# A two-layer hybrid decoder: the last two pairs of a Strassen half multiplied ordinarily, the first up columns interleaved, the right half's chunks one block of K apart

## The chip, the cores and the metric

The kernel runs on one core of one Trainium2 chip. The metric is the device time of one execution in microseconds, 2214.55 in the median of three runs before the change (2214.05 to 2215.54). Engines are called as in the profile: PE is TensorE (matmuls, with PEld its weight loads), DVE is VectorE, ACT is ScalarE, POOL is GpSimd, SP is SyncE, which here only issues DMAs.

## The reference

Two layers, 256 tokens, width 2048, everything in float32. Each layer has a mixer (attention and a short gated convolution, one shared output projection) and an MLP. The change lies in the MLP and at its two ends:

```python
def reference(x, w_in, w_out, ..., w_up, w_down, rel_bias):
    for l in range(DEPTH):                       # 2
        h = _rmsnorm(x, attn_norm_g[l])
        proj = h @ w_in[l]                       # 2048 -> 6144
        ...                                      # attention and gated convolution
        x = x + jnp.concatenate([attn, conv], axis=-1) @ w_out[l]
        hm = _rmsnorm(x, mlp_norm_g[l]) @ w_up[l]             # 2048 -> 8192
        x = x + jnp.square(jax.nn.relu(hm)) @ w_down[l]       # 8192 -> 2048
    return x
```

## The kernel before

**Number format.** Every operand of a product is split into two rounded float32 parts, `hi` (made by ACT) and `lo` = value - hi (made by DVE). A product is three matmuls, hi.hi, hi.lo and lo.hi (`TERMS`). So each block of weights costs a DMA (SP queue), a `whi` or `uhi` on ACT and a `wlo` or `ulo` on DVE before PE can use it. A list of jobs does these (`Weights`): `take()` hands out the next one and makes jobs up to three ahead (`AHEAD`).

**Memory.** x stays in SBUF in four column chunks of 512 (`xs[0..3]`), each with two token tiles. Pools that are opened in a function are laid out in the order of opening and closed at its end; the next function's pools reuse the memory, and what is loaded there waits for the last reader of what lay there before. `mm` holds two PSUM tiles of two banks, `ps` three single banks (`bank`) and one named `av`.

**Order of work.** PE executes in the order of the program. On the other engines, and on the DMA queues, a scheduler orders the instructions by a simulated timeline, except those that `late` pins to their place in the program. Work beside the main stream (norms, transposes `tpn`, `nT`) is cut into pieces by generators (`work`), which advance at `tick()`.

**Mixer, `mixer`.** Projections by `linear` and `linear_t`, 512 output columns at a time, then the output projection "o" (four chunks n), after each of which x is updated (L658) and the MLP's norm is fed: `mnorm.chunk(n, 2)` transposes the chunk of x (`tpn`) and makes the two parts of it, `nT` (L247, L248). The last chunk, 3, is ready only some microseconds after the last matmul of "o".

**MLP, `mlp`.** DFF = 8192 is walked in 32 pairs (`NP`) of two 128-wide blocks of K. For pair i, two up columns (`up_column`, 64 matmuls) give h, [128, 4 blocks of 128]: two K blocks by two token tiles. `evict` adds their two halves, `square` applies relu, the norm's ratio and the square, stores the result to DRAM (`hid`, by the POOL queue), forms the Strassen sums S1 to S4 and splits all eight blocks into `f` (L805 hi, L806 lo). An up column needs all four chunks of `nT`: the first half of K (kh 0) chunks 0 and 1, the second half chunks 2 and 3.

The left half of the output columns (0 to 1023) is made by Strassen's products in Winograd's form, seven per pair of three matmuls 128x512 each instead of eight, accumulated in seven PSUM banks over all pairs. The products of pair j come two pairs (`LAG`) behind its up columns: after the first column of pair i the products of A11, A12, S4 and S1, after the second the other three. Their right-hand sides come from `quarters`: the raw rows of w_down (`draw`, 1024 KB per pair), the parts b1 and b2, the sums t (DVE, L724 to L728), and their parts t13 and t24 (L707 ACT, L708 DVE). All of these but b1 have one buffer.

After the last pair, the seven products are combined into x chunks 0 and 1 (`onto` and four adds, all on DVE). Then the right half (columns 1024 to 2047) is multiplied ordinarily: per pair the squared hidden is loaded back (`back`, 256 KB, SP queue), split (`fr`, L885 and L886), and 24 matmuls `dn` per K block run over both column chunks and both token tiles (L892). Both chunks end with the last pair; then x chunks 2 and 3 are updated and the next layer's norm or the output store follows. The next layer's first projection, q, starts on PSUM that the dn accumulators free.

## Time and profile before

| | |
|---|---|
| median of three runs | 2214.55 us (2214.05 to 2215.54) |
| the profiled execution | 2216.24 us |
| its span | 2214.4 us |
| its mean granted clock | 0.989 |
| matmul instructions | 11054 |
| DMA, mean over the span | 202 GB/s, 446.64 MB |
| `uraw`, 1024 KB, issue to landing | 5.8 us (median) |
| `draw`, 1024 KB | 5.1 us |
| `raw`, 512 KB | 3.6 to 3.9 us |
| `back`, 256 KB | 2.7 us |

The profile is of one execution. Its table of busy time says how long each engine worked; a row of digits per 40th of the span says how the granted clock of PE went; the chain of waits, followed back from the last instruction, says whose work set the end. The table of waits lists, for one engine, which instruction stood idle, for whom, for how long in all, how many times, and the longest. The timeline lists start, duration, engine, line, operation and tile, with the idle time before it and who ended it. The table by stage gives, for a stretch from:to, its length and then the busy time of PE, PEld, DVE, ACT and POOL with the number of instructions, then PE's granted clock, the DMA share and GB/s.

### The profile page before, as it was taken

Reading aid. Unit: us, or ns where it says so; the run is one execution under the profiler, and the core shown is the slowest. Engines: PE = TensorE matmul, PEld = TensorE weight load, DVE = VectorE, ACT = ScalarE, POOL = GpSimd, SP = SyncE. Lnnn points to the kernel's source line nnn. Section 1 sums busy time; section 2 is a strip of 40 time slices with the busy share of each in tenths; the row PEclk is TensorE's granted clock in tenths of the full one; section 3 lists DMA queues with packets and bytes.
Section 4 is the critical chain, followed back from the end, with each engine's and each line's share of the span. In section 5 each row is a group of like instructions: output and inputs, shape, how many; then the busy total and the mean of one; then the engine's idle time right before and its main releaser. Section 6 shows DMA issues by size and latency. Waiting matters only on the chain.

```text
span 2214.4 us, 29244 instructions
## 1 busy us (share of the span) xinstructions
PE 2167.4 (98%) x11054; PEld 1836.7 (83%) x11054; DVE 1631.7 (74%) x2303; ACT 1296.1 (59%) x1758; POOL 130.7 (6%) x186
## 2 busy tenths in 40 slices
PE   8999999999999999799999999999999999998999
PEld 6888888788888888688878888887888888886887
DVE  6677655789898989665556776557989898987555
ACT  6455445566666666454454654446666666664443
POOL 2021200000000000000010111000000000000000
PEclk9999999999999999899999999999999999998999
DMA  7656666566766666477565566656666666665774
GB/s 259 180 153 194 202 185 180 190 218 206 221 211 217 215 212 202 166 234 241 185 191 180 159 197 197 188 164 205 217 212 216 215 213 219 211 198 161 244 244 164
DMA packets 280717, 446.64 MB, mean 202 GB/s; under 512 B 10915, under 2 KB 191733, under 8 KB 280576
## 3 DMA queue, kind: packets, MB, share of 16 engines
q1 hardware_dynamic: 273872, 423.66, 61.7%
q0 software_dynamic: 6656, 21.10, 2.5%
q8 instruction: 86, 1.41, 0.3%
q14 instruction: 55, 0.45, 0.1%
q10 hardware_dynamic: 48, 0.02, 0.0%
HBM read 425.84 MB, written 18.90 MB: 201 GB/s over the span
## 4 chain that ended last, share of the span: by engine, by line
PE 96%; DMA 1%; DVE 1%; ACT 0%; issue 0%; POOL 0%; SPq 0%; DVEq 0%
PE dn L892 16%; PE pr L815 14%; PE o L337 8%; PE gc L359 4%; PE ci L359 4%; PE q L337 4%; PE gb L359 4%; PE v L337 4%; PE k L337 4%; DMA draw<-in_w_down_dram 1%; PE sc L499 1%; PE av L535 1%; PE tpn L401 0%; DVE wlo L282 0%; PE ptp L525 0%; PE up00b L776 0%
## 5 line engine op out<-in xcount | busy, mean ns | idle before, releaser
L282 DVE TENSOR_TENSOR wlo<-raw,whi 128x1024 fp32r<-128x1024 f32 (+1 forms) x258 | 317.1, 1231 | 244.3 <-ACT whi L281 243.1
L281 ACT ACTIVATE whi<-raw 128x1024 fp32r<-128x1024 f32 (+1 forms) x258 | 271.3, 1053 | 311.8 <-PE o L337 73.6
L692 ACT ACTIVATE uhi<-uraw 128x1024 fp32r<-128x1024 f32 x256 | 270.6, 1057 | 304.4 <-PE o L337 10.0
L693 DVE TENSOR_TENSOR ulo<-uraw,uhi 128x1024 fp32r<-128x1024 f32 x256 | 312.6, 1221 | 110.9 <-ACT uhi L692 106.7
L892 PE MATMUL dn<-whi,fr 128*128 128x512 f32 x1024 | 319.9, 393 | 9.5 <-ACT fr L885 7.0
L282 DVE TENSOR_TENSOR wlo<-draw,whi 128x1024 fp32r<-128x1024 f32 x128 | 156.9, 1225 | 150.7 <-ACT whi L281 150.6
L281 ACT ACTIVATE whi<-draw 128x1024 fp32r<-128x1024 f32 x128 | 135.7, 1061 | 174.4 <-PE dn L892 168.4
L892 PEld LDWEIGHTS dn<-whi,fr 128*128 128x128 f32 x1024 | 194.3, 190 | 51.4 <-ACT fr L885 7.9
L892 PE MATMUL dn<-wlo,fr 128*128 128x512 f32 x512 | 200.8, 392 | 0.0
L337 PE MATMUL o<-whi,cat 128*128 128x512 f32 x512 | 159.6, 390 | 0.0
L892 PEld LDWEIGHTS dn<-wlo,fr 128*128 128x128 f32 x512 | 97.2, 190 | 20.1
L337 PEld LDWEIGHTS o<-whi,cat 128*128 128x128 f32 x512 | 96.1, 188 | 19.8
L815 PE MATMUL pr<-t13h,f 128*128 128x512 f32 x256 | 100.5, 395 | 0.0
L337 PE MATMUL o<-wlo,cat 128*128 128x512 f32 x256 | 99.6, 389 | 0.0
L799 POOL DMA_DIRECT2D hid<-h x64 | 34.8, 544 | 985.4 <-ACT h L798 985.4
L815 PE MATMUL pr<-b2h,f 128*128 128x512 f32 x256 | 91.4, 398 | 0.0
L337 PE MATMUL q<-whi,nT 128*128 128x512 f32 x256 | 87.0, 409 | 3.3 <-ACT nT L247 2.1
L815 PE MATMUL pr<-t24h,f 128*128 128x512 f32 x256 | 89.6, 391 | 0.0
L337 PE MATMUL k<-whi,nT 128*128 128x512 f32 x256 | 85.3, 399 | 0.0
L337 PE MATMUL v<-whi,nT 128*128 128x512 f32 x256 | 83.4, 396 | 0.0
L708 DVE TENSOR_TENSOR t24l<-t,t24h 128x1024 fp32r<-128x1024 f32 x64 | 78.4, 1225 | 3.5 <-ACT t24h L707 0.4
L708 DVE TENSOR_TENSOR t13l<-t,t13h 128x1024 fp32r<-128x1024 f32 x64 | 78.4, 1224 | 3.5 <-ACT t13h L707 1.5
(953 smaller groups left out, 4667.8 us busy)
## 6 DMA issues: line engine op xcount, KB each, us to landing
uraw<-in_w_up_dram SPq DMA_DIRECT2D x128, 1024.0 KB, 5.8
draw<-in_w_down_dram SPq DMA_DIRECT2D x128, 1024.0 KB, 5.1
raw<-in_w_in_dram SPq DMA_DIRECT2D x192, 512.0 KB, 3.9
raw<-in_w_out_dram SPq DMA_DIRECT2D x64, 512.0 KB, 3.6
hid<-h POOLq DMA_DIRECT2D x64, 256.0 KB, 3.5
back<-hid SPq DMA_DIRECT2D x64, 256.0 KB, 2.7
rev<-by_dist_d POOLq DMA_DIRECT2D x4, 1024.0 KB, 10.6
out_dram<-x SPq DMA_DIRECT2D x8, 256.0 KB, 2.3
```

What stands on the lines that cost most here:

```text
L281: nc.scalar.activation(hi[:, k], raw[:, k], AF.Copy)
L282: nc.vector.tensor_sub(lo[:, k], raw[:, k], hi[:, k].bitcast(F32))
L337: nc.tensor.matmul(acc[:, t], a.ap[:, pa, k % KG, t * P:(t + 1) * P], (hi, lo)[pw][:, j], start=(k == 0 and n == 0), stop=(k == nk - 1 and ...
L359: nc.tensor.matmul(acc[:, f, 0] if part else acc[:, f], wt[:, k % 4, fs], a.ap[:, 0, k % KG] if part else a.ap[:, :, k % KG], start=(part ...
L499: nc.tensor.matmul(sc[:, :W], qT[m * DK:(m + 1) * DK, a, i, t * P:(t + 1) * P], kT[m * DK:(m + 1) * DK, b, i, :W], start=(n == 0), stop=(n ...
L535: nc.tensor.matmul(av[:, i * P:(i + 1) * P], pT[:, a, k * P:(k + 1) * P], v[:, b, k, i * P:(i + 1) * P], start=(k == 0 and n == 0), stop=( ...
L692: nc.scalar.activation(hi, src, AF.Copy)
L693: nc.vector.tensor_sub(lo, src, hi.bitcast(F32))
L708: nc.vector.tensor_sub(lo, src, hi.bitcast(F32))
L799: nc.gpsimd.dma_start(hid[i], u)
L815: nc.tensor.matmul(prods[n], f[:, pa, a], b[pw], start=(i == 0 and m == 0), stop=(i == NP - 1 and m == 2))
L892: nc.tensor.matmul(acc[n][:, t], f[:, pa, k, t * P:(t + 1) * P], b[pw][:, n], start=(i == 0 and k == 0 and m == 0), stop=(i == NP - 1 and ...
```

## The change

Three parts of `mlp` are changed, and with them the order in which its pools are opened.

1. The Strassen products take pairs 0 to 29 only. Pairs 30 and 31 are multiplied ordinarily, 48 matmuls for both, accumulated onto the banks of products 2, 4 and 3, which hold parts of one output block alone, and onto a free bank (product 8, the up columns' `av`). Their `f` has four blocks instead of eight, with no sums S1 to S4, and their rows of w_down go through `rows` and the ordinary weights, without t, t13, t24. Products 1, 5, 6 and 7 are combined while these matmuls run; four adds go from DVE to POOL.
2. The right half runs over 16 blocks of four K blocks (`NB2`), chunk n = 1 one block behind n = 0 (`order`). `hid` and `back` are 512 KB, the weights come as 512-column loads of 512 KB, as in the mixer, and each chunk's x update and norm start when it ends. The pools for it, `rpool` and `gpool`, are opened where `spool` and `upool` are closed.
3. Pair 0's two up columns run side by side, on one `mm` tile: first half of K for both, then the second half for both. Pair 1 uses two single banks, one for each column.

Besides, `fpool` and `dpool` are opened first, `spool` and `upool` last, and everything that `quarters(0)` makes on ACT and DVE after its DMA is pinned (`keep`).

```diff
-            upool = scope.enter_context(tc.tile_pool(name="upool", bufs=3))
-            spool = scope.enter_context(tc.tile_pool(name="spool", bufs=1))
             fpool = scope.enter_context(tc.tile_pool(name="fpool", bufs=2))
             dpool = scope.enter_context(tc.tile_pool(name="dpool", bufs=2))
+            first = scope.enter_context(ExitStack())
+            spool = first.enter_context(tc.tile_pool(name="spool", bufs=1))
+            upool = first.enter_context(tc.tile_pool(name="upool", bufs=3))
...
-            weights = Weights(upool)
+            weights = Weights(None)
...
+                keep = late if i == 0 else lambda ins: None
...
+                    keep(nc.scalar.activation(hi, src, AF.Copy))
+                    keep(nc.vector.tensor_sub(lo, src, hi.bitcast(F32)))
...
-                    nc.vector.tensor_sub(t[:, 0:2], raw[:, :, 1], raw[:, 0])
+                    keep(nc.vector.tensor_sub(t[:, 0:2], raw[:, :, 1], raw[:, 0]))
...
+                    keep(nc.vector.tensor_add(t[:, 2], t[:, 1], raw[:, 0, 0]))
+                    keep(nc.vector.tensor_sub(t[:, 3], raw[:, 1, 0], t[:, 2]))
...
-                        box.append(load_rows(i, 2 * CH))
+                        box.append(load_rows(i, 0))
...
-            for i in range(NP + LAG):
-                plain, sums, more = quarters(i - LAG)
-                if i < NP:
-                    column(i, 0, 0)
-                    column(i, 0, 1)
-                if i >= LAG:
-                    weights.jobs += [plain, sums]
-                if i < NP:
-                    column(i, 1, 0)
-                    column(i, 1, 1)
-                if i >= LAG:
-                    weights.jobs.append(more)
             for i in range(NP):
+                pair = quarters(i - LAG)
+                if i == 0:
+                    for kh in range(2):
+                        for c in range(2):
+                            column(0, c, kh)
+                    continue
+                for c in range(2):
+                    column(i, c, 0)
+                    column(i, c, 1)
+                    if i >= LAG:
+                        weights.jobs += (pair[2:], pair[:2])[c == 0]
+            for i in range(NP - LAG, NP):
                 box = []
                 rows(i, 0, box)
                 rows(i, 1, box)
...
-            hid = [dram.tile([P, 2 * S], F32, name=f"hid{l}{i}") for i in range(NP)]
-            def up_column(name, warm):
...
+            order = [(b - n, n) for b in range(NB2 + 1) for n in range(2) if 0 <= b - n < NB2]
+            for b, n in order:
+                weights.straight(w_down[l], b * KG * P, KG, (2 + n) * CH)
+            hid = [dram.tile([P, KG * S], F32, name=f"hid{l}{b}") for b in range(NB2)]
...
+                nc.gpsimd.dma_start(hid[i // 2][:, i % 2 * 2 * S:(i % 2 + 1) * 2 * S], u)
+                n = 4
+                if i < NP - LAG:
+                    n = 8
...
-                nc.vector.tensor_sub(f[:, 1], h, f[:, 0].bitcast(F32))
+                nc.scalar.activation(f[:, 0, :n], h[:, :n], AF.Copy)
+                nc.vector.tensor_sub(f[:, 1, :n], h[:, :n], f[:, 0, :n].bitcast(F32))
...
-            h = None
-            for i in range(NP + LAG):
+            for i in range(NP):
                 j = i - LAG
-                if i < NP:
-                    h = fpool.tile([P, 8, P], F32, tag="h", name="h", bufs=1)
-                    evict(up_column(f"up{l}{i}a", i < LAG),
-                          h[:, 0:2].rearrange("p a c -> p (a c)"))
...
-                if j >= 0:
-                    b11, b21, b22 = weights.take()
-                    t1, t3 = weights.take()
-                    product(0, j, A11, b11)
-                    product(1, j, A12, b21)
-                    product(2, j, S4, b22)
-                    product(4, j, S1, t1)
-                    work.tick()
-                if i < NP:
...
+                end = i == NP - 1
+                h = fpool.tile([P, 8, P], F32, tag="h", name="h", bufs=1)
+                if i == 0:
+                    two = mm.tile([P, 2, CH], F32, tag="mm2", name="up0")
+                    two = [two[:, c].rearrange("p (h s) -> p h s", h=2) for c in range(2)]
+                    for kh in range(2):
+                        for c in range(2):
+                            up_part(two[c], kh)
+                            if kh:
+                                evict(two[c], h[:, 2 * c:2 * c + 2])
+                    fs[0] = square(0, h)
+                    continue
+                for c in range(2):
+                    if i < LAG:
+                        acc = bank("upw").rearrange("p (h s) -> p h s", h=2)
+                    else:
+                        acc = column_bank()
+                    up_part(acc, 0)
+                    up_part(acc, 1)
+                    evict(acc, h[:, 2 * c:2 * c + 2])
+                    if c == 1:
+                        fs[i] = square(i, h)
+                    if j == 0 and c == 0:
+                        for pair in ((1, 6), (2, 3)):
+                            w2 = mm.tile([P, 2, CH], F32, tag="mm2", name=f"pr{l}{pair[0]}")
+                            prods[pair[0]], prods[pair[1]] = w2[:, 0], w2[:, 1]
+                        for n in (4, 5, 7):
+                            prods[n] = bank(f"pr{l}{n}")
+                    if j >= 0 and c == 0:
+                        b11, b21, b22 = weights.take()
+                        t1, t3 = weights.take()
+                        product(1, j, A11, b11, end)
+                        product(2, j, A12, b21)
+                        product(3, j, S4, b22)
+                        product(5, j, S1, t1, end)
+                        work.tick()
+                    elif j >= 0:
+                        t2, t4 = weights.take()
+                        product(7, j, S3, t3, end)
+                        product(6, j, S2, t2, end)
+                        product(4, j, A22, t4)
+                        work.tick()
+            first.close()
+            rpool = scope.enter_context(tc.tile_pool(name="rpool", bufs=RAW))
+            gpool = scope.enter_context(tc.tile_pool(name="gpool", bufs=3))
+            weights.pool = rpool
+            def block(b):
+                back = gpool.tile([P, KG * S], F32, tag="back", name="back", bufs=2)
+                nc.sync.dma_start(back, hid[b])
+                f = gpool.tile([P, 2, KG, S], F32R, tag="g", name="g")
+                flat = f.rearrange("p a k s -> p a (k s)")
+                nc.scalar.activation(flat[:, 0], back, AF.Copy)
+                nc.vector.tensor_sub(flat[:, 1], back, flat[:, 0].bitcast(F32))
+                return f
+            blocks = {0: block(0)}
...
-            e1 = wide("e1")
-            nc.scalar.activation(e1, p1, AF.Copy, scale=mnorm.scale)
-            onto(xs[0][:, 0], p2, xs[0][:, 0])
-            onto(xs[1][:, 0], p3, xs[1][:, 0])
-            onto(xs[0][:, 1], p4, xs[0][:, 1])
-            u2, u3, u4 = wide("u2"), wide("u3"), wide("u4")
-            onto(u2, p6, e1)
-            onto(u3, p7, u2)
-            onto(u4, p5, u2)
-            onto(xs[1][:, 1], p5, xs[1][:, 1])
-            for dst, v in ((xs[0][:, 0], e1), (xs[1][:, 0], u4), (xs[0][:, 1], u3),
-                           (xs[1][:, 1], u3)):
-                nc.vector.tensor_add(dst, dst, v)
+            x11, x21, x12, x22 = (xs[n][:, t] for n in range(2) for t in range(NT))
+            e1, e2, e3, e4 = wide("e1"), wide("e2"), wide("e3"), wide("e4")
+            nc.scalar.activation(e1, prods[1], AF.Copy, scale=mnorm.scale)
+            onto(e2, prods[6], e1)
+            onto(e4, prods[5], e2)
+            onto(x22, prods[5], x22)
+            onto(e3, prods[7], e2)
+            for dst, v in ((x11, e1), (x12, e4), (x21, e3), (x22, e3)):
+                nc.gpsimd.tensor_tensor(dst, dst, v, op=ALU.add)
+            prods[8] = ps.tile([P, CH], F32, tag="av", name=f"pr{l}8", bufs=1)
+            for j in range(NP - LAG, NP):
+                for k in range(2):
+                    b = weights.take()
+                    for n, t, p in ((0, 0, 2), (0, 1, 4), (1, 0, 3), (1, 1, 8)):
+                        for m, (pa, pw) in enumerate(TERMS):
+                            nc.tensor.matmul(
+                                prods[p], fs[j][:, pa, 2 * k + t], b[pw][:, n],
+                                start=(p == 8 and j == NP - LAG and k == 0 and m == 0),
+                                stop=(j == NP - 1 and k == 1 and m == 2))
+                    work.tick()
+            for dst, p in ((x11, 2), (x21, 4), (x12, 3), (x22, 8)):
+                onto(dst, prods[p], dst)
...
             if last:
-                for n in range(2):
-                    for t in range(NT):
-                        nc.sync.dma_start(
-                            out[0, t * P:(t + 1) * P, n * CH:(n + 1) * CH], xs[n][:, t])
+                store(0)
+                store(1)
             else:
                 work.start(norm.chunk(0, 2), 12)
...
-            acc = [mm.tile([P, NT, CH], F32, tag="mm2", name=f"dn{l}{n}") for n in range(2)]
-            for i in range(NP):
-                back = nat.tile([P, 2, S], F32, tag="wide", name="back")
-                nc.sync.dma_start(back.rearrange("p k s -> p (k s)"), hid[i])
-                f = fpool.tile([P, 2, 2, S], F32R, tag="f", name="fr")
-                nc.scalar.activation(f[:, 0], back, AF.Copy)
-                nc.vector.tensor_sub(f[:, 1], back, f[:, 0].bitcast(F32))
-                for k in range(2):
-                    b = weights.take()
-                    for n in range(2):
+            accs = {}
+            for b, n in order:
+                if n == 0:
+                    if b + 1 < NB2:
+                        blocks[b + 1] = block(b + 1)
+                if b == 0:
+                    accs[n] = mm.tile([P, NT, CH], F32, tag="mm2", name=f"dn{l}{n}")
+                f, acc = blocks[b], accs[n]
+                for kp in range(KG // 2):
+                    hi, lo = weights.take()
+                    for k in (2 * kp, 2 * kp + 1):
                         for t in range(NT):
                             for m, (pa, pw) in enumerate(TERMS):
                                 nc.tensor.matmul(
-                                    acc[n][:, t], f[:, pa, k, t * P:(t + 1) * P], b[pw][:, n],
-                                    start=(i == 0 and k == 0 and m == 0),
-                                    stop=(i == NP - 1 and k == 1 and m == 2))
+                                    acc[:, t], f[:, pa, k, t * P:(t + 1) * P],
+                                    (hi, lo)[pw][:, k % 2],
+                                    start=(b == 0 and k == 0 and m == 0),
+                                    stop=(b == NB2 - 1 and k == KG - 1 and m == 2))
                         work.tick()
-            for n in range(2):
-                for t in range(NT):
-                    onto(xs[2 + n][:, t], acc[n][:, t], xs[2 + n][:, t])
+                if b == NB2 - 1:
+                    for t in range(NT):
+                        onto(xs[2 + n][:, t], acc[:, t], xs[2 + n][:, t])
                     if last:
-                        nc.sync.dma_start(
-                            out[0, t * P:(t + 1) * P, (2 + n) * CH:(3 + n) * CH],
-                            xs[2 + n][:, t])
-                if not last:
-                    work.start(norm.chunk(2 + n, 2))
+                        store(2 + n)
+                    else:
+                        work.start(norm.chunk(2 + n, 2))
```

## The prediction

> **What bounds the kernel now.** I read the page first: which engine is busy, and whether its clock ever drops.
>
> ```profile
> PE 2167.4 (98%) x11054; PEld 1836.7 (83%) x11054; DVE 1631.7 (74%) x2303; ACT 1296.1 (59%) x1758; POOL 130.7 (6%) x186
> PEclk9999999999999999899999999999999999998999
> PE 96%; DMA 1%; DVE 1%; ACT 0%; issue 0%; POOL 0%; SPq 0%; DVEq 0%
> ```
>
> TensorE carries the end (96% of the chain). Time is lost only where PE waits, and just after, when its granted clock is low (the 8s). So next the waits of PE (total, times, longest):
>
> ```profile
> PE pr L815 <- ACT f L805: 9.8, 2, 5.0
> PE dn L892 <- ACT fr L885: 7.0, 2, 5.6
> PE up00a L776 <- DVE nT L248: 4.7, 2, 3.7
> PE up10a L776 <- DVE nT L248: 4.6, 2, 3.6
> PE tpn L401 <- DVE nT L248: 3.0, 1, 3.0
> PE dn L892 <- DVE fr L886: 2.5, 1, 2.5
> PE pr L815 <- DVE t24l L708: 2.3, 2, 1.1
> ```
>
> Almost all lie at three places per layer: the first up columns, the end of the left half, the layer boundary. The table by stage (from:to, length, then PE busy; the clock stands after POOL):
>
> ```profile
> 398.97:418.27 19.30, 14.60 (x75) 12.39 (x74) 17.33 (x28) 12.07 (x19) 0.89 (x2) 0.82 0.83 272
> 905.41:940.02 34.61, 22.86 (x74) 16.88 (x72) 23.79 (x32) 16.07 (x24) 0.54 (x1) 0.75 0.58 203
> 1111.39:1141.34 29.95, 25.85 (x115) 21.31 (x115) 16.52 (x25) 15.27 (x26) 3.32 (x5) 0.94 0.68 211
> 1502.01:1520.91 18.90, 14.35 (x76) 12.18 (x74) 17.20 (x28) 12.09 (x19) 0.89 (x2) 0.91 0.83 278
> 2008.04:2038.04 30.00, 19.66 (x64) 14.12 (x63) 22.83 (x31) 12.44 (x15) 0.54 (x1) 0.77 0.56 177
> ```
>
> Everywhere else (940.02 to 1111.39: busy 171.37 of 171.37, clock 1.00) PE is full. Unit prices at full clock: 0.2267 us per 128x512 matmul (612 dn in 138.75 us). After an idle of some 5 us (918.64, 932.52, 2021.50) matmuls start 0.43 us apart for 5.7 to 6.3 us, which loses about 2.9 us; after 2.5 to 3.7 us of idle, 1 to 1.5 us.
>
> **1. Tail of the left half: -17.3 and -14.5 us.** From the last up matmul of layer 1 to its last dn matmul the trace has 905.41 to 1111.39, 205.98 us. Content: 9+21+21 = 51 product matmuls, 768 dn, 16 transposes of 0.1 = 11.6 + 174.1 + 1.6 = 187.3. So 18.7 us are lost: waits of 1.14, 4.80, 0.25 and 5.55, and about 7 at low clock. In layer 2, 201.59 against 185.7 (no transposes): 15.9 lost. The change makes pairs 30 and 31 cost 48 matmuls instead of 42, +1.4 us, and takes the sums and the 1024-wide `f` out ahead of them. I count from T, the last up matmul: nine products end at 2.05, pair 30 lasts to 7.5. Meanwhile ACT does `ev` 0.58, `e1` 0.58, relu and square 0.62 each, half an `f` hi 0.6; DVE, in the built order, `h` 0.4, `e2`, the ratio, `e4`, `x22`, `e3` (0.75 each) and half an `f` lo, 0.68: ready at about T+6, 1.5 before pair 31. The SP queue can't issue `back` and the first right-half weights before the last Strassen product (their buffers reuse its memory): T+2.25; 512 KB land in 3.6 to 3.9; `g` hi 6.5 to 7.5, the last `whi` of pair 31 to 8.5, its `wlo` 8.7 to 9.9, needed at 10.2 to 10.5. First right-half weights: ready 11.05, needed 12.97. So nothing waits, if those landings hold; gain 18.7 - 1.4 and 15.9 - 1.4. Were the dn wait to stay with its slow clock (5.55+2.9), -9 would remain per layer: the other bound.
>
> Four adds go to POOL, and POOL can cost DVE time:
>
> ```profile
> 233.78 1.29 POOL L645 TENSOR_TENSOR gc02w<-gc02w,rowb 128x512 f32<-128x512 f32 x1
> 234.10 2.05 DVE L282 TENSOR_TENSOR wlo<-raw,whi 128x1024 fp32r<-128x1024 f32 x1 [0.83 <-ACT whi L281]
> ```
>
> A `wlo` that takes 1.22 alone takes 2.05 beside a 1.29 us POOL operation. POOL's last add would run till T+8.3, beside `g` lo: +0.8, so pair 31's last `wlo` ends at 10.7 and not 9.9, and PE waits 0.3: +0.3 per layer (bounds 0 and 1.9, all four at 0.83 less the 1.5 of slack). The Trainium skill (GPSIMD Engine Reference, Specifications) puts such contention on DVE instructions with two SBUF inputs; then `e2` to `e3`, which read PSUM, are spared. The trace agrees: a 0.68 us add from PSUM at 232.59 kept 0.68 beside a POOL operation. Were they not spared, `f` lo would be 2.5 us later, and each layer would pay 1 more.
>
> **2. Right half one block apart: -6.0 us, once.** In layer 1's boundary, 29.95 us hold waits of 1.10 (PSUM of q, behind the x update of 2.72) and 3.00 (`tpn` for nT), 4.1, and 1.9 of low clock. Chunk 0 now ends a block (48 matmuls, 10.9 us) before chunk 1, and so do its x update, its norm pieces and its PSUM. The next q's first weights can be issued at the last `wlo`, some 6.6 us before the last dn; landing 3.8, `whi` 1.06, `wlo` 1.22: ready 0.5 early. Content remains: -6.0 (bounds 0, if that 0.5 fails, and -6.0). At the end of the kernel the last x update and store remain: 0.
>
> **3. First up columns side by side: +4.4 and +4.7 us.** The order of columns alone would hide the wait for nT chunk 3:
>
> ```profile
> 398.97 1.98 PE L776 MATMUL up00a<-nT,uhi 128*128 128x512 f32 x8
> 404.69 0.50 PE L776 MATMUL up00a<-nT,uhi 128*128 128x512 f32 x1 [0.98 <-DVE nT L248]
> 408.91 1.65 PE L776 MATMUL up00a<-nT,uhi 128*128 128x512 f32 x3 [3.72 <-DVE nT L248]
> 399.21 0.88 SPq L699 DMA_DIRECT2D draw<-in_w_down_dram  x2
> 393.73 1.06 ACT L692 ACTIVATE uhi<-uraw 128x1024 fp32r<-128x1024 f32 x1 [1.66 <-PE o L337]
> ```
>
> Waits 0.98 + 3.72 and 2.4 at low clock: 7.15 of 19.30, so content 12.15 (layer 2: 6.75 of 18.90). But the diff also reverses the pools. In before, `uraw` lies where the mixer's bias lay, is loaded at 205 us, and `uhi` is made at 393.73, under the o projection; it is `draw` that waits for the last o matmul (399.21). In the built program of the changed kernel `dpool` and `upool` have swapped places: `uraw` overlaps the mixer's `cat`, and its first DMA waits for the last o matmul. All SP issues behind it wait too, the next two `uraw` among them. So: issue 399.2, landing 6.2 (as the draw issued there; bounds 5.4, the fastest, and 8.4, the median of uraw at 395 to 425), `uhi` 1.06, first up matmul 406.5 instead of 398.97: 7.6 us idle, 2.9 of low clock, 0.8 because column 1 ends in the tile that column 0's eviction reads, 0.2 for nT: 12.15 + 11.5 = 23.65 (layer 2 alike), against 19.30 and 18.90. Bounds +2.3 and +6.6.
>
> **4. Pair 0's quarters pinned: +9.9 us in each layer.** `t` and `t13` of pair 0 were made at 405 to 411 us, far ahead of use. `keep` now holds them in program order, and in the built order DVE's `t` stands behind `b2l` and `f` lo of pair 1. `b2l` needs `b2h` of pair 1 (one buffer), which waits for pair 0's product 3. But `t13` is needed directly after product 3. From X, the end of up column 2a: product 3 ends 2.2, `b2h` 3.3, `b2l` 4.5, `f` lo 5.6, `t` 6.9, `t13h` 7.95, `t13l` 9.2. PE, in order, waits from 2.05 to 7.98 and again to 9.2, and the next up column starts at 9.7 and not 2.73: 7.0 idle and 2.9 of low clock. DVE and ACT, held up likewise, catch up in the slow stretch. Bounds: 7.0 (no low clock) and 11 (`t24` late too).
>
> The 2.9 is a row. The Trainium skill (TensorE: Matmul & The Clock Gate, Part 1) has the gate release after one busy window of about 3.4 us at half rate, 1.7 lost per idle: the four new idles would then cost 4.8 less, 2201. The trace has 5.7 to 6.3 us.
>
> **Sum.** -17.3 - 14.5 + 0.6 - 6.0 + 4.4 + 4.7 + 9.9 + 9.9 = -8.3. The profiled execution took 2216.24 (span 2214.4): 2207.9. The median of the runs is 2214.55, 1.7 lower: 2206.
>
> **Rivals.**
> (a) Neither start stall comes (the reused memory and the pinned order bite nowhere). For it: none of these waits is in this trace. Against it: both orders stand in the built program. Then part 4 is 0 and part 3 is -6.3 and -5.9 (the waits less 0.85): 2216.2 - 37.2 - 12.2 - 1.7 = 2165.
> (b) One of the two comes: without part 4, 2206 - 19.8 = 2186; without part 3's late uraw, 2206 - 21.3 = 2185.
> (c) Slower than before: the right half becomes bound by transfers. Its weights now come in rows of 512 columns instead of 1024. A layer's right half moves 33.5 MB of weights and 8.4 of hidden in 174.1 us, 241 GB/s. Loads of such rows ran at 179 GB/s with a DMA share of 0.63 (1141 to 1160), full share 284; the present ones at 217 with 0.68, full 319. That speaks against it, with 0.85 of the limit used. It decides below 41.9/(174.1+6.4) = 232 GB/s, where the two layers' extra passes 8.3 + 4.4; at 230 it costs 8.1 per layer, 2222.
> (d) The change does not do what it says, the tail's waits return (`back` late): -9 per layer, 2206 + 14 = 2220.
>
> **How the numbers follow.** Forecast 0.55, own range 2195 to 2218 (gate and landing low; landing high and one tail wait). (a) 0.10, (b) 0.17, (c) 0.10, (d) 0.08. Two of ten may fall outside 2182 to 2224: it leaves out (a) and the far ends of (c). No change means within 0.2%, 4.4 us, which a measurement here can just tell: under 2210.1 is faster, over 2219 slower. Faster: 0.40 of the forecast's 0.55, (a), and nearly all of (b): 0.65. Slower: (c), most of (d), little of the forecast: 0.17. Same: 0.18.
>
> **What would show it.** Part 1: no PE wait on `f` or `g` behind the last up column, at most 0.3 on a `wlo`. Part 2: no wait on nT between the layers. Part 3: first `uraw` issued right behind the last o matmul, first up matmul waiting some 7.6 us for `uhi`. Part 4: product 5 of pair 0 waiting about 6 us for `t13h` and 1.2 for `t13l`. A wait of dn on `whi` or `raw` all through the right half means (c). If `uraw` loads before the last o matmul, or if `t13` is ready in time, I am wrong by 20 us.

## The result and the profile after

The changed kernel takes 2212.18 us in the median of 16 runs (2209.88 to 2214.07), beside 2215.67 in 16 runs of the kernel before (2214.05 to 2218.11) on the same chips. The ratio is 0.9984, 95% interval 0.9976 to 0.9991. So it is faster by 3.5 us, 0.16%: clear of zero by the interval, but inside the 0.2% that the prediction called no change (its line for faster was 2210.1), an outcome to which it gave 0.18. The profiled execution took 2213.11, with a span of 2211.3; the forecast for it was 2207.9.

Span by stage. "Front" is the end of the o projection to the end of pair 0's two up columns (64 matmuls), "loop" reaches to the last up column, "tail" to the last dn matmul. "Boundary" is the start of the next layer's q projection, its first 96 matmuls, up to the first k:

| stage | before | after | forecast | measured |
|---|---|---|---|---|
| start | 398.97 | 398.26 | 0 | -0.7 |
| front, layer 1 | 19.30 | 24.85 | +4.4 | +5.6 |
| loop, layer 1 | 487.14 | 497.70 | +9.9 | +10.6 |
| tail, layer 1 | 205.98 | 190.85 | -17.0 | -15.1 |
| boundary | 29.95 | 23.15 | -6.0 | -6.8 |
| mixer 2 | 360.67 | 360.82 | 0 | +0.2 |
| front, layer 2 | 18.90 | 25.47 | +4.7 | +6.6 |
| loop, layer 2 | 487.13 | 497.11 | +9.9 | +10.0 |
| tail, layer 2 | 201.59 | 188.13 | -14.2 | -13.5 |
| end | 4.77 | 4.96 | 0 | +0.2 |

The measured column adds up to -3.1, the difference of the spans. Each stage moved the way that was forecast for it; some 36 us were won and 33 were lost. On the page the shares of the engines have hardly changed, and PE still carries the chain; "issue" has 4% of it, where before it had none:

```profile
PE 2163.5 (98%) x11066; PEld 1835.1 (83%) x11066; DVE 1610.7 (73%) x2229; ACT 1286.7 (58%) x1718; POOL 137.8 (6%) x194
PEclk9999999999999999999999999998999999999999
PE 94%; issue 4%; DMA 1%; DVE 0%; POOL 0%; ACT 0%; SPq 0%; DVEq 0%; POOLq 0%
```

The waits of PE after (total, times, longest) tell more than the shares:

```profile
PE up L789 <- ACT uhi L694: 18.5, 2, 9.6
PE pr L829 <- ACT t13h L714: 11.5, 2, 5.8
...
PE pr L829 <- DVE t13l L715: 3.1, 2, 2.0
PE q L338 <- ACT nT L248: 2.7, 1, 2.7
PE pr L916 <- DVE wlo L283: 1.5, 2, 0.8
PE up L789 <- ACT ev L799: 1.4, 2, 0.7
```

None of the seven waits shown of before is left: `f`, `fr`, the `nT` at the front and the `tpn` at the boundary are gone, but for 0.2 us at the front. (The `q` wait on `nT` is at the start of the kernel.) In their place stand two waits per layer that before did not have: the first up column on `uhi`, and pair 0's fifth product on `t13`.

The stages by window after (from:to, length; busy time of PE, PEld, DVE, ACT, POOL with counts; granted clock, DMA share, GB/s):

```profile
398.26:423.11 24.85, 15.03 (x75) 12.42 (x75) 11.76 (x20) 10.31 (x16) 0.89 (x2) 0.79 0.75 240
436.90:460.00 23.10, 16.23 (x69) 13.15 (x69) 17.87 (x24) 10.86 (x14) 0.56 (x1) 0.78 0.50 153
920.81:934.86 14.05, 13.29 (x59) 10.63 (x58) 13.16 (x13) 8.46 (x11) 5.64 (x5) 1.00 0.74 268
934.86:1111.66 176.80, 176.80 (x793) 146.63 (x792) 102.57 (x97) 89.56 (x102) 0.00 (x0) 1.00 0.72 229
1111.66:1134.81 23.15, 23.15 (x108) 19.22 (x106) 14.65 (x20) 12.23 (x18) 3.35 (x5) 1.00 0.90 298
```

The tail and the boundary (the last three rows) are now all but full: PE waits 0.76 us in them, at clock 1.00. The first two rows are where the gain went: the front, with a clock of 0.79, and the stretch around pair 0's products, where PE now waits and the clock is 0.78.

The front in the timeline (start, length, engine, line, operation; in brackets the idle time before it and what ended it), SP and ACT first, then PE:

```profile
398.49 16.50 SPq L687 DMA_DIRECT2D uraw<-in_w_up_dram  x5
...
406.28 2.00 ACT L694 ACTIVATE uhi<-uraw 128x1024 fp32r<-128x1024 f32 x2 [5.77 <-DMA uraw<-in_w_up_dram]
...
398.03 0.39 PE L338 MATMUL o<-whi,cat 128*128 128x512 f32 x1
407.39 3.78 PE L789 MATMUL up<-nT,uhi 128*128 128x512 f32 x8 [8.98 <-ACT uhi L694]
...
420.21 2.12 PE L789 MATMUL up<-nT,uhi 128*128 128x512 f32 x8 [0.69 <-ACT ev L799]
```

The first `uraw` is issued right behind the last o matmul, as forecast, and lands 7.7 us later. And pair 0's products in layer 1:

```profile
443.23 1.22 DVE L715 TENSOR_TENSOR b2l<-draw,b2h 128x1024 fp32r<-128x1024 f32 x1 [0.86 <-ACT b2h L714]
444.37 1.22 DVE L821 TENSOR_TENSOR f<-h,f 128x1024 fp32r<-128x1024 f32 x1
445.51 1.22 DVE L728 TENSOR_TENSOR t<-draw 128x1024 f32<-128x1024 f32 x1
...
446.76 1.06 ACT L714 ACTIVATE t13h<-t 128x1024 fp32r<-128x1024 f32 x1 [2.62 <-DVE t L728]
...
447.87 0.79 PE L829 MATMUL pr<-t13h,f 128*128 128x512 f32 x1 [5.76 <-ACT t13h L714]
449.76 0.80 PE L829 MATMUL pr<-t13l,f 128*128 128x512 f32 x1 [1.10 <-DVE t13l L715]
450.78 3.62 PE L789 MATMUL upc<-nT,uhi 128*128 128x512 f32 x8
```

`t` is the third in DVE's queue, behind `b2l` and `f` lo of pair 1, and PE stands for 5.76 and 1.10 us in front of `t13h` and `t13l`. The prediction wrote these steps as offsets from the start of pair 0's products, X, which is 439.87 here: `t13h` needed from X+2.05 and there at X+7.98, which is 447.85.

### The profile page after: what moved, and what is told of

It is laid out like the page before. It is cut to its first block, busy times and chain, and to the rows that moved or that the text cites. A ratio compares the mean times of both kernels' runs of the same rounds, so it can differ in the third digit from the quotient of the medians.

```text
span 2211.3 us, 29293 instructions
## 1 busy us (share of the span) xinstructions
PE 2163.5 (98%) x11066; PEld 1835.1 (83%) x11066; DVE 1610.7 (73%) x2229; ACT 1286.7 (58%) x1718; POOL 137.8 (6%) x194
## 3 DMA queue, kind: packets, MB, share of 16 engines
HBM read 425.84 MB, written 18.90 MB: 201 GB/s over the span
## 4 chain that ended last, share of the span: by engine, by line
PE 94%; issue 4%; DMA 1%; DVE 0%; POOL 0%; ACT 0%; SPq 0%; DVEq 0%; POOLq 0%
PE upc L789 30%; PE dn L950 16%; PE pr L829 13%; PE o L338 8%; PE q L338 4%; PE gc L360 4%; PE ci L360 4%; PE gb L360 4%; PE v L338 4%; PE k L338 4%; PE sc L500 1%; PE av L536 1%; DMA hid<-h 1%; DMA raw<-in_w_down_dram 1%; PE tpn L402 1%
## 5 line engine op out<-in xcount | busy, mean ns | idle before, releaser
L283 DVE TENSOR_TENSOR wlo<-raw,whi 128x1024 fp32r<-128x1024 f32 (+1 forms) x386 | 473.4, 1227 | 384.2 <-ACT whi L282 382.8
L282 ACT ACTIVATE whi<-raw 128x1024 fp32r<-128x1024 f32 (+1 forms) x386 | 407.2, 1055 | 481.1 <-PE dn L950 163.6
L789 PE MATMUL upc<-nT,uhi 128*128 128x512 f32 x1920 | 480.2, 392 | 0.0
L789 PEld LDWEIGHTS upc<-nT,uhi 128*128 128x128 f32 x1920 | 354.9, 189 | 69.0
L950 PE MATMUL dn<-whi,g 128*128 128x512 f32 x1024 | 316.3, 389 | 0.0
L789 PEld LDWEIGHTS upc<-nT,ulo 128*128 128x128 f32 x1920 | 262.8, 191 | 18.8
L789 PE MATMUL upc<-nT,ulo 128*128 128x256 f32 x1920 | 268.5, 283 | 0.0
L950 PEld LDWEIGHTS dn<-whi,g 128*128 128x128 f32 x1024 | 192.2, 188 | 40.0
L950 PE MATMUL dn<-wlo,g 128*128 128x512 f32 x512 | 199.2, 389 | 0.0
L950 PEld LDWEIGHTS dn<-wlo,g 128*128 128x128 f32 x512 | 96.1, 188 | 19.8
L829 PE MATMUL pr<-t13h,f 128*128 128x512 f32 x240 | 95.1, 396 | 11.5 <-ACT t13h L714 11.5
```

The source lines that it names most:

```text
L282: nc.scalar.activation(hi[:, k], raw[:, k], AF.Copy)
L283: nc.vector.tensor_sub(lo[:, k], raw[:, k], hi[:, k].bitcast(F32))
L789: nc.tensor.matmul(acc[:, 0] if part else acc, wt[:, k], a.ap[:, 0, k % KG] if part else a.ap[:, :, k % KG], start=(part == 0 and kh == 0 ...
L829: nc.tensor.matmul(prods[n], fs[j][:, pa, a], b[pw], start=(j == 0 and m == 0), stop=(stop and m == 2))
L950: nc.tensor.matmul(acc[:, t], f[:, pa, k, t * P:(t + 1) * P], (hi, lo)[pw][:, k % 2], start=(b == 0 and k == 0 and m == 0), stop=(b == NB2 ...
```

## The experiments

Every run was timed beside the kernel before in the same group; ratios are to that kernel, with 95% intervals. Diffs are against the changed kernel. The expectations, which were written before each run, call the runs by short names, in the order of the work: e1 is the pin taken away, e2 the old layout of the pools with the pin left in, e3 and e4 both undone (columns side by side, then one after the other), e5 pair 0 one pair earlier, e6 two `uraw` buffers, e7 the adds on DVE, e8 the chunks in the same block, e9 and e11 another layout in both orders, e10 the draws held back, e12 both stalls avoided.

### The pin of pair 0 taken away

```diff
-                keep = late if i == 0 else lambda ins: None
+                keep = lambda ins: None
```

> The changed kernel without `keep`: pair 0's quarters may be made ahead again. My theory (product 5 of pair 0 waits 5.8 and 1.1 us for t13 in the changed kernel, and the stretch from pair 1's first column to the end of the last up column is 10.6 and 10.0 us longer than before): both waits go, the stretch returns to some 487 us per layer, and the time is about 20 us below the changed kernel, 24 below the kernel before (2192). Rival: the wait belongs to the one buffer of b2 and t13, and comes back somewhere in the first pairs: within 5 us of the changed kernel.

2194.39 us, ratio 0.9903 [0.989, 0.9917]. Both waits on `t13` are gone. The loops take 487.13 and 487.14, as before the change; fronts 25.03 and 26.25 and tails 190.83 and 188.10 stay. So the pin costs 10.6 and 10.0 us a layer, and buys nothing in this layout, where the first `uraw` is late anyway. (Of these 20.6 us, 17.8 reached the median: the start of this profiled run was 1.5 us longer and its second front 0.8.)

### The pools laid out as before, the pin left in

```diff
-            fpool = scope.enter_context(tc.tile_pool(name="fpool", bufs=2))
-            dpool = scope.enter_context(tc.tile_pool(name="dpool", bufs=2))
+            fpool = scope.enter_context(tc.tile_pool(name="fpool", bufs=2, side="right"))
+            dpool = scope.enter_context(tc.tile_pool(name="dpool", bufs=2, side="right"))
...
-            spool = first.enter_context(tc.tile_pool(name="spool", bufs=1))
             upool = first.enter_context(tc.tile_pool(name="upool", bufs=3))
+            spool = first.enter_context(tc.tile_pool(name="spool", bufs=1))
```

> The changed kernel with `upool` and `spool` laid where the kernel before has them and `fpool`, `dpool` at the other end of the memory: the first `uraw` loads no longer reuse the mixer's `cat`. `keep` stays. My theory: the first up matmul follows the last o matmul at once, the front falls from 24.9 and 25.5 us to about 13.2 each, and the time is about 24 us below the changed kernel, 27 below the kernel before (2188). Rival: the idle at the front is due to nT chunk 3 and the norm as before: the front keeps some 19 us, and the time falls by 12 at most.

2206.73 us, ratio 0.9957 [0.9944, 0.9971]. The fronts fall to 14.85 and 14.55, 10 and 11 us less: the late `uraw` is the layout's doing. But only 5.5 us of the 21 reached the end, so the theory's 2188 was missed; the total fell by no more than the rival's 12, though not for its reason, a front that stays at 19. The boundary grew to 32.80 (+9.65), with a new 5.3 us wait of `q` on `whi`: the same pools, closed at the end of the left half, decide what memory the right half gets, and its `back` and `g` now lay over the next mixer's first weight buffers, whose load therefore waited for the last dn. Tails grew by 1.1 each, loops by 2. The layout only moved the wait to another place.

### Both undone, and the columns one after the other

The first of these has both edits above. The second, besides, walks the columns in the order of before:

```diff
-                    for kh in range(2):
-                        for c in range(2):
+                    for c in range(2):
+                        for kh in range(2):
```

> Both edits at once: no `keep`, and `uraw` in its old place. If the two stalls are separate, their gains add: 44 us below the changed kernel, 48 below the kernel before (2168). Rival: without the pin, pair 0's sums get ahead of the first columns' `ulo` on DVE as soon as these are early, and the front gives back 2 to 5 us per layer: 2172 to 2178.

> As e3_both, with pair 0's two up columns one after the other again (first c, then kh). My theory: the second half of K of the first column then waits for nT chunk 3, 0.98 and 3.7 us with some 2.4 at low clock, as in the kernel before: 6 us per layer more than e3_both, 12 in all (2180). Rival: what the side-by-side order saves is lost to the extra wait for the first eviction (0.7) and to DVE: within 3 us of e3_both.

2204.46 (0.9949 [0.9936, 0.9961]) and 2199.84 (0.993 [0.9917, 0.9942]). The gains do not add: without the pin the fronts are 22.24 and 22.22. The trace of the first shows what the pin is for (DVE's queue, then PE, around the front):

```profile
414.11 1.22 DVE L728 TENSOR_TENSOR t<-draw 128x1024 f32<-128x1024 f32 x1 [5.08 <-DMA draw<-in_w_down_dram]
415.25 0.48 DVE L249 SCALAR_TENSOR_TENSOR nT<-tpn,gains,nT 128x256 fp32r<-128x256 f32 x1
...
415.79 0.80 PE L789 MATMUL up<-nT,uhi 128*128 128x512 f32 x1 [5.44 <-DVE nT L249]
```

DVE, in order, stands 5.08 us before a `t` whose `draw` hasn't landed, and the last piece of `nT`, which PE needs, is queued behind that `t`. The pin keeps `t` out of the way here (fronts 14.85 and 14.55 with it, 22.24 and 22.22 without), at the price of 10 us where `t` is needed. Theory and rival both put the first total far too low (2168, and 2172 to 2178). Nor did the order of the columns do what the theory said (2180 for the second, 12 above the first): side by side is 4.6 us slower. But the two runs don't isolate the order. Its fronts are only 1.8 and 0.4 us longer than the 20.49 and 21.84 of the other, and 2.7 us of the difference stand ahead of the first front (a start of 401.15, against 398.46), in a part that the edit doesn't touch. The loads, too, left in another order: side by side, one `uraw` leaves at 400.98 and the draws behind it at 401.52, the first of which lands at 414.09; one after the other, the draws leave first, at 398.70, the first lands at 404.66, and `t` doesn't wait. What the order of the columns itself is worth in this layout is not shown.

### Pair 0's weights made one pair earlier, and a gap between the pools

The old layout again, 20 KB left free ahead of the right half's pools, and the jobs of pair 0 issued during pair 1's first column (pin kept):

```diff
+                    if i == 1 and c == 0:
+                        weights.jobs += quarters0[:2]
...
+            gap = scope.enter_context(tc.tile_pool(name="gap", bufs=1))
+            gap.tile([P, 5 * KG * S], F32, tag="gap", name="gap")
```

> e2_old_pools with two more edits: `rpool` and `gpool` start 20 KB higher, where the next mixer's weight buffers are free early (e2 lost 9.7 us at the layer boundary to a q load that waited for the last dn), and pair 0's b1, b2, t and t13 stay pinned but are made one pair earlier, during pair 1's columns. My theory, all from stages already measured: front 14.9 as in e2, loop some 488 as in e3, boundary 23.2 as in the changed kernel, tail 191: about 35 us below the changed kernel, 38 below the kernel before (2177). Rival: DVE can't do pair 0's sums and the first columns at once wherever they stand; the nT wait of e3 (5.4 and 5.6, with low clock some 8 per layer) or the t13 wait stays: 2193.

2195.3 us, ratio 0.9908 [0.9893, 0.9922]. No wait on `t13` is left, and the fronts are 14.57 and 13.97. A new wait of 4.6 us per layer stands in the loop, of an up column on its eviction; the timeline of ACT shows the cause:

```profile
444.35 0.63 ACT L714 ACTIVATE b1h<-draw 128x512 fp32r<-128x512 f32 x1 [3.67 <-DMA draw<-in_w_down_dram]
444.88 0.58 ACT L802 ACTIVATE ev<-upc 128x512 f32<-128x512 f32 x1
```

The eviction `ev` waits in ACT's order behind a `b1h` whose `draw` was issued late, at 434.20, when pair 0's `t` had freed one of the two buffers, and landed 10.1 us later, behind a `uraw` issued just ahead of it. The total is near the rival's 2193, but not for its reason: neither the `nT` wait nor that on `t13` stayed. The gap lay in the wrong place: the boundary is 32.13, its 5.3 us wait unchanged.

### Is the late first load a matter of how many are under way?

Two loads of `uraw` instead of three, and then the two `draw` loads pinned behind them:

```diff
-            upool = first.enter_context(tc.tile_pool(name="upool", bufs=3))
+            upool = first.enter_context(tc.tile_pool(name="upool", bufs=2))
```

```diff
-                nc.sync.dma_start(
+                (late if i < 2 else lambda ins: None)(nc.sync.dma_start(
```

> The changed kernel with two `uraw` buffers instead of three, so that two and not three 1 MB loads leave together behind the last o matmul. My theory: the landing of the first, 7.7 us against the 6.2 that I took from two draws issued together, is a share of the bandwidth among all that left together; it falls to about 6.2, and the idle at the front from 9.0 and 9.6 to about 7.5. Later loads may be late, so the total may be anything from 4 us faster to 10 slower; the idle is what tells. Rival: the landing belongs to the place or to the first use of that memory: idle unchanged within 0.4.

> The changed kernel with the `draw` loads of pairs 0 and 1 pinned to their place in the program, so that they leave behind six `uraw` loads instead of 6 us ahead of the first. e6 left the idle at the front at 8.5 and 9.3, so the number of `uraw` loads that leave together does not set the landing. My theory now: the two draws, 2 MB, are still in the air when the first `uraw` is issued (they land 7.1 us after issue), and without them the first lands in 5.8 (the median of all) and the idle falls by about 2, to 7 and 7.5. Rival: rows of 1 KB, which a `uraw` has and a `draw` (4 KB) has not, make the landing 7.7 even alone: idle unchanged within 0.5.

With two buffers, 2225.13 (1.0044 [1.0027, 1.0061]): PE still idles 8.50 and 9.33 us at the front, so a third `uraw` explains 0.5 and 0.2 us of the idle time and no more; later columns lose the buffer. With the draws held back, 2223.54 (1.0035 [1.0021, 1.0049]); SP's queue and ACT at the front:

```profile
400.44 1.96 SPq L687 DMA_DIRECT2D uraw<-in_w_up_dram  x3
...
407.28 2.00 ACT L694 ACTIVATE uhi<-uraw 128x1024 fp32r<-128x1024 f32 x2 [4.83 <-DMA uraw<-in_w_up_dram]
```

The first `uraw` lands in 6.7 us in both layers, instead of 7.7 and 8.3 in the changed kernel, and the idle time is 8.04 and 8.00, where the five kernels with the draws ahead in this layout (the changed one, the one without the pin, the one with two buffers, and the two further below with the adds on DVE and the chunks in one block) have 8.40 to 9.56. So the draws ahead of it in the queue cost 0.4 to 1.5 us of idle time, and most of the stall comes from the load's late start and its own landing. In the changed kernel the second draw was still in the air for 2.7 us after the `uraw` was issued (393.06 to 401.24). The idle time fell by 0.9 and 1.6 of the theory's 2 us; why the first still takes 6.7 and not the 5.8 of the median is not shown. Holding the draws back moved the stall: PE's wait for pair 0's `t13h` grew from 5.76 to 11.5 and 13.0 us, and the loops by 4.9 and 7.4.

### The four adds on DVE instead of POOL

```diff
-                nc.gpsimd.tensor_tensor(dst, dst, v, op=ALU.add)
+                nc.vector.tensor_add(dst, dst, v)
```

> The changed kernel with the four adds of the tail on DVE instead of POOL. My theory: the `g` lo that took 3.47 us beside two POOL adds takes 1.22 again, and the wait of 0.76 for pair 31's last `wlo` changes by less than a us, since the adds cost DVE about what POOL took from it (2.7 against 2.25): total within 2 us of the changed kernel. Rival: `g` lo is slow for another reason (its `back`, DMA traffic) and keeps 3.4, and the wait grows by the adds, 2.7 per layer.

2210.82 us, ratio 0.9977 [0.9966, 0.9987]; its interval overlaps the changed kernel's. First the end of the left half in the changed kernel, DVE, POOL and PE:

```profile
927.54 3.47 DVE L891 TENSOR_TENSOR g<-back,g 128x1024 fp32r<-128x1024 f32 x1
...
927.36 2.55 POOL L908 TENSOR_TENSOR x<-x,e 128x512 f32<-128x512 f32 x2
...
932.19 0.50 PE L916 MATMUL pr<-wlo,f 128*128 128x512 f32 x1 [0.76 <-DVE wlo L283]
```

And the same `g` lo with the adds on DVE:

```profile
929.84 1.22 DVE L891 TENSOR_TENSOR g<-back,g 128x1024 fp32r<-128x1024 f32 x1
```

`g` lo takes 3.47 us beside 2.55 us of POOL and 1.22 alone, and the 0.76 us wait of PE is gone. The four adds take 0.68 each on DVE and come before `g` lo, which so starts 2.3 us later; counted from the start of the product stage it ends 9.5 us in, against 10.2: the product stage is 0.67 shorter (13.38, not 14.05), but the stretch up to q 0.46 longer (why is left open). So the tails win only 0.2 to 0.3.

### The right half's chunks in the same block

```diff
-            order = [(b - n, n) for b in range(NB2 + 1) for n in range(2) if 0 <= b - n < NB2]
+            order = [(b, n) for b in range(NB2) for n in range(2)]
```

> The changed kernel with the right half's two chunks in the same block, n = 0 then n = 1, so that chunk 0 ends 24 matmuls (5.4 us) before chunk 1 and not 48. My theory: PSUM and x update of chunk 0 are still free in time, but the norm's pieces of chunks 2 and 3 come closer together: 0 to 3 us more at the layer boundary, 23 to 26. Rival: the 6.8 us gained at the boundary hang on the full block: the boundary returns to about 30.

2212.41 us, ratio 0.9986 [0.9977, 0.9996]. The boundary is 23.92 instead of 23.15, with one wait of 0.33. Of the 6.8 us that part 2 won, a whole block between the chunks is worth 0.8: that chunk 0 ends 24 matmuls (5.4 us) ahead of chunk 1 is enough for the rest.

### Another layout, with both orders of the columns

`dpool` where the mixer's bias was, `uraw` behind it, `fpool` at the other end, and a gap that puts the right half's weights on the next mixer's first buffers; no pin. The second walks the columns one after the other.

```diff
-            fpool = scope.enter_context(tc.tile_pool(name="fpool", bufs=2))
+            fpool = scope.enter_context(tc.tile_pool(name="fpool", bufs=2, side="right"))
...
-            spool = first.enter_context(tc.tile_pool(name="spool", bufs=1))
             upool = first.enter_context(tc.tile_pool(name="upool", bufs=3))
+            spool = first.enter_context(tc.tile_pool(name="spool", bufs=1))
...
-                keep = late if i == 0 else lambda ins: None
+                keep = lambda ins: None
...
+            gap = scope.enter_context(tc.tile_pool(name="gap", bufs=1))
+            gap.tile([P, 3 * KG * S], F32, tag="gap", name="gap")
```

> The changed kernel without `keep` and with another layout: `draw` lies where the mixer's bias was (loaded long ahead), `uraw` behind it (its first tile free at once, the others when the last w_out loads are converted), `fpool` at the far end, `rpool` exactly where the next mixer's loads want to be. So neither load waits for the last o matmul, and no q load for the last dn. My theory: loop 487 and boundary 23.2 as in e1_no_pin, front 13 to 16 instead of 24.9: some 19 us below e1_no_pin (2175, 41 below the kernel before). Rival: with all of pair 0's data there early, DVE makes b1, b2 and t of pair 0 ahead of `ulo` and nT chunk 3 (about 6 us of work), and the front keeps a wait of 3 to 5 with low clock: 18 to 21 per front, 2182 to 2188.

> e9_lay with pair 0's two up columns one after the other. My theory: what the side-by-side order is for, hiding nT chunk 3 behind the first half of K of both columns (5.6 us of matmuls), shows here: 3 to 6 us per layer slower than e9_lay. Rival: nT chunk 3 is late by more than those 5.6 us hide or DVE's own order decides, as e3 against e4 (12 us apart in the other direction, 22.3 and 20.5 in the front): equal or faster.

2203.2 (0.9946 [0.9932, 0.9959]) and 2203.91 (0.9945 [0.9933, 0.9958]). The boundary is good again (23.17, 23.13), so the old readers of the right half's memory were its cause. But the fronts are worse, 27.86 and 28.34 in the first, 28.07 and 28.54 in the second, with 8.4 us before `rbc`, and the totals are far from the 2175 of the theory and the rival's 2182 to 2188. DVE's queue in the first:

```profile
402.56 1.21 DVE L728 TENSOR_TENSOR t<-draw 128x1024 f32<-128x1024 f32 x1
403.69 1.22 DVE L695 TENSOR_TENSOR ulo<-uraw,uhi 128x1024 fp32r<-128x1024 f32 x1
404.83 0.68 DVE L715 TENSOR_TENSOR b1l<-draw,b1h 128x512 fp32r<-128x512 f32 x1
405.43 1.22 DVE L715 TENSOR_TENSOR b2l<-draw,b2h 128x1024 fp32r<-128x1024 f32 x1
```

With the draws early and no pin, DVE makes the weights of pairs 0 and 1 ahead of the `nT` and the `ulo` that PE stands waiting for. With such a queue the order of columns decides nothing: the two agree within 1 us.

### Both stalls avoided

Pair 0 one pair earlier (as above), a third `draw` buffer, `g` first, `back` in a pool of its own, and the right half's weights exactly on the mixer's first buffers (a 4 KB gap):

```diff
-            dpool = scope.enter_context(tc.tile_pool(name="dpool", bufs=2))
+            dpool = scope.enter_context(tc.tile_pool(name="dpool", bufs=3, side="right"))
...
-            rpool = scope.enter_context(tc.tile_pool(name="rpool", bufs=RAW))
...
+            gap = scope.enter_context(tc.tile_pool(name="gap", bufs=1))
+            gap.tile([P, KG * S], F32, tag="gap", name="gap")
+            rpool = scope.enter_context(tc.tile_pool(name="rpool", bufs=RAW))
+            kpool = scope.enter_context(tc.tile_pool(name="kpool", bufs=2))
```

> e5_gap_early0 mended in the two places where its trace shows new waits: a third `draw` buffer, so that pair 2's load needs no longer wait for pair 0's sums (e5 lost 4.6 us and low clock per layer, ACT standing on that load ahead of an eviction), and `rpool` exactly where the next mixer's first loads want to be (e5 still lost 5.3 and low clock at the layer boundary). `uraw` lies early as in e2, the pin stays, pair 0's quarters are made one pair earlier. If the changed kernel's loss is those stalls and nothing else: front 14.6, loop 488, tail 191, boundary 23.2, in all some 22 us below e5: 2173, 43 below the kernel before. Rival: a stall taken away comes back at the next load in the queue, as in e3, e5 and e9: between 2180 and 2195.

2180.11 us (2175.67 to 2180.96), ratio 0.9834 [0.9821, 0.9847]: 36 us faster than before the change, and the best kernel here. PE's busy line of its page, and its waits behind the start of the kernel:

```profile
PE 2157.9 (99%) x11066; PEld 1829.2 (84%) x11066; DVE 1603.4 (74%) x2229; ACT 1273.1 (59%) x1718; POOL 140.1 (6%) x194
```

```profile
PE up L792 <- ACT ev L802: 1.9, 2, 1.2
PE rbc L436 <- DVE diag L433: 1.1, 2, 0.5
PE upc L792 <- ACT ev L802: 1.0, 1, 1.0
PE pr L924 <- DVE wlo L283: 1.0, 2, 0.5
PE q00tp L478 <- DVE q00n L469: 0.7, 1, 0.7
PE q L338 <- DVE wlo L283: 0.7, 1, 0.7
```

It executes the same 11066 matmuls as the changed kernel; none of these waits is over 1.2 us. Fronts 13.97 and 14.45, loops 488.72 and 490.02, tails 190.87 and 188.11, boundary 24.18. So the gains of the changed kernel can be had without its four stalls. Of the profiled runs' 38.4 us (2214.4 to 2176.0 in span), the tails bring 28.6, the boundary 5.8, the fronts 5.3 and 4.5, and 5.7 are lost again, 1.6 and 2.9 in the loops and 1.2 at the start. The total is at the low edge of the rival's range (2180 to 2195), not at the theory's 2173: small waits did come back.

## Why the prediction was right and wrong

The direction held, if barely, each of the waits that were forecast came at its place, and none of the rivals came. The gain was mis-sized: 5.2 us too much for the profiled execution (2207.9 forecast, 2213.11 measured). The forecast was the small rest of +28.9 and -37.2, so an error of 5 was more than half of it. By stage, the fronts came out 3.0 us worse than forecast, the tails 2.6, the loops 0.7, mixer and end 0.3; the boundary came out 0.8 better, and the start, which the change doesn't touch, 0.7. That the sum is off by no more is in part luck.

**Part 3 is the step that failed, by 3.0 of the 5.2 us.** The landing of the first `uraw`, "6.2 (as the draw issued there)", took 7.7 and, in layer 2, 8.3; the bounds 5.4 to 8.4 held both. So the idle time was 8.98 and 9.56, not 7.6. The 6.2 was the landing of a draw with nothing ahead of it in the queue; here two draws of 1 MB were issued some 6 us ahead and still in the air. Holding them back took 0.9 and 1.6 us off the landing; the 0.5 that remain beyond 6.2 are not explained. Two smaller errors of the part nearly cancel. The content of pair 0's two columns is 12.76, not 12.15: in the last experiment they take 13.98 from the end of o, of which 0.53 and 0.69 are waits. (The low clock in the front before had so cost 1.8, not 2.4.) And what the low clock lost is 15.03 - 12.76 = 2.3 us (layer 2: 15.23 - 12.76 = 2.5), not 2.9. The eviction's wait was 0.69, for 0.8.

**Part 1, tails: -15.1 and -13.5, forecast -17.0 and -14.2.** No wait on `f`, `g` or `fr` came back, and (d) fell. The wait from POOL's contention is 0.76 and 0.78, where 0.3 was forecast: the two last adds run together as 2.55 us beside `g` lo, and slow it by 2.25, not by 0.8. Of the 1.9 us missing in layer 1, 0.9 were only booked wrongly. Its dn stage holds 24 transposes, not 16 (2.7 us beyond 768 matmuls at 0.2267, so 0.11 each): with chunk 0 a block ahead, its transposes move from the boundary into the tail. Some 0.5 us remain unexplained.

**Part 2, boundary: -6.8, forecast -6.0.** The 0.8 beyond the forecast is mostly those eight transposes (0.11 each). That the next q's weights would be there 0.5 us early held: PE is busy in all of the 23.15 us. The step was right in its sum, but the full block was not what won it.

**Part 4, the pin: +10.6 and +10.0, forecast +9.9 each**, confirmed by taking it away. Both waits came as worked out (5.76 for X+7.98 minus X+2.05 = 5.93; 1.10 in layer 1 and 1.97 in layer 2 for 1.2).

**The rivals.** (a) and (b): both stalls came. (b)'s price for the first, 2186, is 8 below the 2194 that the kernel without the pin measures: mostly the front and tail errors above. Its price for the other, 2185, is 22 below the 2207 of the old layout with the pin, because that layout moved the wait to the boundary. (c): the dn stage is busy in 176.80 of 176.80 us at a DMA share of 0.72. What comes nearest to (a)'s kernel is the last experiment: 2180, not 2165, since its fronts keep waits of 0.5 to 1.2 us, its loops are 1.6 and 2.9 longer than before, and the terms of parts 1 to 3 that it used were too good by the errors above.

**The clock.** In every trace here the granted clock changes only at the edges of windows of 3.41 us, which follow one another without a gap, and it returns to 1.00 at the end of the first window that PE filled or nearly filled. Windows of the changed kernel (PE's busy time, granted clock):

| window | at | PE busy, us | clock |
|---|---|---|---|
| 404.79 to 408.21 | front, layer 1, PE starts at 407.39 | 0.82 | 0.50 |
| 408.21 to 411.62 | | 3.41 | 0.50 |
| 411.62 to 415.03 | | 3.41 | 1.00 |
| 445.75 to 449.16 | pair 0's products, layer 1, PE starts at 447.87 | 0.79 | 0.50 |
| 449.16 to 452.57 | the rest of the wait of 1.10 falls here | 2.81 | 0.50 |
| 452.57 to 455.98 | | 3.41 | 0.50 |
| 455.99 to 459.40 | | 3.41 | 1.00 |
| 1544.85 to 1548.26 | the same in layer 2, PE starts at 1545.85 | 0.80 | 0.50 |
| 1548.26 to 1551.67 | the rest of the wait of 1.97 falls here | 3.05 | 0.50 |
| 1551.67 to 1555.08 | | 3.41 | 1.00 |

So the low clock after a restart lasted for the rest of the window into which the restart fell and one window more: 4.2 us (from 407.39), 5.5 (from 1505.19) and 5.8 (from 1545.85). At pair 0 in layer 1 the wait of 1.10 us left only 2.81 us of work in the second window, a third was needed, and it lasted 8.1. In all the traces, low windows with up to 2.81 us of work were followed by another, those with 2.83 or more by full clock. Lost were 2.3 and 2.5 us at the fronts; the loops lost 10.56 - 6.86 = 3.7 and 9.98 - 7.73 = 2.25 beyond their idle time. If all of this is the clock's, the four come to 10.7, near the 11.6 of the prediction's row and far from four times the 1.7 of its other reading, 6.8.

But the row's 2.9 is no constant: by these windows an idle without a second wait costs, as an estimate, from 1.7 us (half of one window) to 3.4 (half of two), and where in the window the restart falls decides. The Trainium skill (TensorE: Matmul & The Clock Gate, Part 1) has such a window of about 3.4 us, and it has the window run on whatever the kernel does. The trace agrees; the 1.7 is what it gives for a restart at a window's start. When the clock drops is not shown here as cleanly.

## What to carry to other kernels

The order and lifetime of memory pools decide whose last reader the next stage's first load waits for: here 10 us per layer at one place, and after a naive repair 10 us at another, so look at what lies under a buffer both when it is opened and when it is closed. A pin that keeps work out of a busy queue has a price where that work is next needed; with the first `uraw` early, the kernel took 2206.73 us with the pin, 2204.46 without it, and 2195.3 with the pinned work started a pair earlier; a third `draw` buffer and a better place for the right half's pools brought it to 2180.11. And where large gains and losses nearly cancel, each term has to be known to a microsecond before the sign and size of the rest mean much: take a landing from the load that really stands there, with what is queued ahead of it (7.7 and 8.3 us here, where a load with nothing ahead had taken 6.2).

## What the runs showed of the hardware

- A DVE operation with two SBUF inputs can be stopped for nearly the whole of a POOL operation beside it: 3.47 us beside 2.55 of POOL adds, 1.22 without (2.25 of 2.55 lost). That DVE operation started later than POOL's (927.54 and 927.36). Where DVE started first, it was POOL that stood: in the kernel before, a POOL add of 128x512, of a size that took 1.29 us at 233.78, took 4.42 at 229.41, beside three `wlo` (from 229.18) that took no longer than 1.22 each. The sums of DVE that read PSUM kept 0.73 to 0.75 beside a POOL add of 1.31 (925.54 on). The Trainium skill (GPSIMD Engine Reference, Specifications) names the same instructions as those that contend, and the trace agrees.
- The granted clock changed only at the edges of windows of 3.41 us, and came back after the first window that PE had nearly filled (2.83 us of work sufficed, 2.81 did not). So the low clock after an idle time did not grow with its length: 4.2 and 5.5 us of it after 9.0 and 9.6 us of idle, 8.1 after 5.76 and, inside the next window, 1.10.
- The boundary runs at a DMA share of 0.90 and 298 GB/s without one wait of PE, more than the 0.72 and 229 GB/s of the dn stage that rival (c) feared for.
